# Four feed-forward chunks instead of two projected up by seven products, and one low part of each second pair formed by VectorE

## The chip, the cores and the metric

The kernel runs on one core of a Trainium2 chip. The core has TensorE (PE in the rows of the profile) for matrix products into PSUM, VectorE (DVE), ScalarE (ACT) and GpSimd (POOL) for element-wise work, and DMA queues that SyncE (SP), ScalarE and GpSimd start. Each engine works through its own instructions in program order and waits for the others on semaphores. The metric is the device time of one execution in microseconds (us), the median over several runs; lower is better.

## The reference

The program is a trunk of two layers over a sequence of 512 tokens with 1024 channels, all in float32. Each layer is wrapped by two feed-forward networks (FFNs), so the program has four of them:

```python
def swiglu_ffn(x, w_gu, w_d):
    g, u = jnp.split(x @ w_gu, 2, axis=-1)
    return (jax.nn.silu(g) * u) @ w_d
...
for i in range(DEPTH):                       # DEPTH = 2
    x = layer_norm(DN_ALPHA * x + 0.5 * swiglu_ffn(x, ffn1_wgu[i], ffn1_wd[i]), ...)
    mix = mlstm_mixer(...) if i % 2 == 0 else gmlp_mixer(...)
    x = layer_norm(DN_ALPHA * x + mix, ...)
    x = layer_norm(DN_ALPHA * x + 0.5 * swiglu_ffn(x, ffn2_wgu[i], ffn2_wd[i]), ...)
    ...                                      # gated per-layer embedding, one more layer_norm
```

The hidden width is 2816, that is 22 blocks of 128. The up projection `x @ w_gu` makes a gate block and an up block of columns for each hidden block; the down projection takes the product back to 1024 channels. Only the FFNs are touched here.

## The kernel before

**Products.** Each float32 operand is split into a high part (rounded to the matmul format, `whi`, by ScalarE, L274) and a low part (`wlo`, the rest). A product is three matmuls: high by high, high by low, low by high (`mm3`, L387 to L389; L389 takes the low part of the weights in the up projection and the low part of `h` in the down projection).

**Chunks.** `ffn` walks over the hidden blocks in six chunks of 2, 4, 4, 4, 4 and 4 blocks (`FFN_CHUNKS`); they are called chunk 0 to chunk 5 below. While a chunk is projected up, the chunk before it is projected down; the down projection always goes by seven products of half-size pieces (`Group`, tile `gps`), whose results are added to the residual `xt` by VectorE (L760, L762) at each step.

**Two ways up.** Chunks 0 to 3 are projected up plainly (tile `sup` in the staged beginning, `fps` after it): for each of the 8 column blocks of a four-block chunk 8 x 3 matmuls of 512 columns. ScalarE's and VectorE's work for one column block is a split of its weights (high on ACT, low on DVE at L283), and after it the SiLU or the product with the gate. Chunks from `UP_FROM` = 4 on go by seven products (`UpForms`, `UpPair`, tile `ups`): two hidden blocks make a pair, a pair is a 2 by 2 arrangement (gate and up columns by two halves of the channels), and seven products of 24 matmuls with 256 columns take the place of eight, after Strassen and Winograd. A chunk has a first and a second pair, so products 0 to 13; after each odd one comes a `gps` product of the down projection.

**What the seven products need.** On the side of the activations seven combinations of quarters of x are formed once for an FFN (tiles `x_a`, `x_f`, `x_d`, `t`, `t_f`, all on VectorE with splits by ScalarE). This is done in the chunk before the first chunk that uses them, two steps after each column block from the third on (`FORM_AT` = 2). On the side of the weights each pair needs four VectorE sums or differences in place (L139, L140 for the third product, L147, L148 for the fifth), on quarters of 512 KB that SyncE loads into `wbox`.

**Low parts.** Of a pair's seven low parts five are made by a DMA (`UP_BY_DMA` = 1, 3, 4, 5, 6): ScalarE writes minus the rounded weights into `wlo` (L280) and a DMA that GpSimd issues (L281) adds the weights to it. The third of them, number 4, is that of the fifth product, whose form is made at L147 and L148. The other two low parts are VectorE subtractions (L289 in these chunks). They are put off: `fill` makes the high part and leaves the low part in `pending`, and `lows` issues it one product later.

**Order.** The order is written out by hand: `W.order` lists the weights in the order of use, `fill` splits the next one when one of four `main` buffers is released after a product, and each engine's program is what these calls emit. A load into a freed quarter waits for the low part that was the quarter's last reader.

**Affine in chunk 1.** Where the norm ahead of an FFN left its gain and shift for later (FFN 2, 3 and 4, not FFN 1), VectorE applies them to `xt` at L754 and L755, once at the end of chunk 0 and three times in the first steps of chunk 1.

Of the kernel before, what the change touches and what calls it, by code (L numbers as in the profile page):

```python
# [17 lines left out]
P = 128  # L18
# [5 lines left out]
HID = 2816  # L24
# [19 lines left out]
EXTRA = 2  # L44
PLE_EXTRA = 3
UP_BY_DMA = (1, 3, 4, 5, 6)


class Weights:
# [75 lines left out]
        self.after.update({t2: (made[0][1],), t1: (made[1][1], t2)})  # L125
        return [(kind, js, make) for js, make in made]

    def up_forms(self, j11, j12, j21, j22):

        vec, raws = self.nc.vector, self.raws  # L130

        def a11():
            return raws[j11], ()

        def a12():
            return raws[j12], ()

        def s2():
            vec.tensor_add(raws[j21], raws[j21], raws[j22])  # L139
            vec.tensor_sub(raws[j11], raws[j21], raws[j11])  # L140
            return raws[j11], ()

        def s1():
            return raws[j21], (j21,)

        def s3():
            vec.tensor_sub(raws[j12], raws[j12], raws[j11])  # L147
            vec.tensor_sub(raws[j11], raws[j22], raws[j11])  # L148
            return raws[j11], (j11,)

        def s4():
            return raws[j12], (j12,)

        def a22():
            return raws[j22], (j22,)

        made = [((j11,), a11), ((j12,), a12), ((j21, j22), s2), ((), s1), ((), s3), ((), s4), ((), a22)]
        for _, make in made:
            self.in_place.add(make)
        self.after.update({s2: (a11,), s3: (a12, s2)})  # L160
        self.by_dma.update(made[r][1] for r in UP_BY_DMA)
        return [("main", js, make) for js, make in made]

    def spare(self, kind):
# [192 lines left out]
def hybrid_trunk(ctx: ExitStack, tc, x, p, ln_g, ln_b, ffn1_wgu, ffn1_wd, ffn2_wgu, ffn2_wd,  # L357
# [87 lines left out]
    def kp(w):  # L445
        return w.rearrange("(kb p) c -> p kb c", p=P)
# [4 lines left out]
    def add_pairs(w, a0, b0):  # L451

        W.add((w_cols(w, a0), cols2), (w_cols(w, b0), cols2))
# [4 lines left out]
    def add_rows(w, kb, n, kind="main"):  # L458
        for k in range(0, n, 2):
            W.add((kp(w)[:, kb + k:kb + k + 2, :], rows2), kind=kinds_of(kind, k))  # L460
# [7 lines left out]

    FFN_CHUNKS = [2, 4, 4, 4, 4, 4]
    LAST = len(FFN_CHUNKS) - 1  # L470
    UP_FROM = 4
    FORM_AT = 2
    turn_p = []

    def ffn_weights(wgu, wd, name, ple=False):
        starts = [sum(FFN_CHUNKS[:c]) for c in range(LAST + 1)]

        def forms(c):
            m = FFN_CHUNKS[c] // 2

            def quarter(i, j):
                k = starts[c] + m * i
                return kp(wd)[:, k:k + m, j * 512:(j + 1) * 512]
            loads = [W.add_load(quarter(i, j), n, name) for i, j, n in ((0, 0, 2), (0, 1, 1), (1, 1, 1), (1, 0, 2))]
            return W.forms("rows", *((j, slice(None)) for j in loads))

        first = len(W.order)
        for at in range(starts[UP_FROM]):
            if at == 0 or at == starts[UP_FROM] - 1:
                W.add(*((kp(wgu)[:, :, c0:c0 + P], [slice(None)]) for c0 in (at * P, HID + at * P)))  # L490
            elif at % 2:
                add_pairs(wgu, at * P, HID + at * P)
        tiles = W.order[first:]
        del W.order[first:]
        for c, n in enumerate(FFN_CHUNKS):
            down_w = deque(forms(c - 1) if c else ())
            if c >= UP_FROM:
                products = []
                for b in range(starts[c], starts[c] + n, 2):
                    products += W.up_forms(*(W.add_load(kp(wgu)[:, k:k + 4, c0:c0 + 2 * P], 1, "box")  # L500
                                             for c0 in (b * P, HID + b * P) for k in (0, 4)))
                for s, product in enumerate(products):
                    W.order.append(product)
                    if s % 2:
                        W.order.append(down_w.popleft())
                continue
            for i in range(2 * n):
                W.order.append(tiles[2 * starts[c] + i])
                if down_w:
                    W.order.append(down_w.popleft())  # L510
        if ple:
            W.add_hook("rows", lambda hi, lo: turn_p.pop()(hi, lo))
        add_rows(wd, starts[LAST], 4, ["rowsx", "rows", "main", "main"] if ple else ["main", "rows", "rowsx", "rows"])
# [74 lines left out]
    def ple_weights(i):  # L588
        add_rows(ple_wp[i], 0, 2)
        add_wide(ple_wg[i], 0, ["extra", "extra", "extra", "main"])  # L590
        add_wide(ple_wg[i], 512, ["rows", "rows", "rowsx", "rows2"])

    ffn_weights(ffn1_wgu[0], ffn1_wd[0], (0, 0))
    ml_weights()
    ffn_weights(ffn2_wgu[0], ffn2_wd[0], (0, 2), True)
    ple_weights(0)
    ffn_weights(ffn1_wgu[1], ffn1_wd[1], (1, 0))
    gm_weights()
    ffn_weights(ffn2_wgu[1], ffn2_wd[1], (1, 2), True)
# [108 lines left out]
    class Norm:  # L708
# [18 lines left out]
        def prepare(self, t):  # L727
            mv = small.tile([P, 2], F32, name="mv", tag="mv")
            vec.bn_aggr(mv, self.st[t])
            rs = small.tile([P, 2], F32, name="rs", tag="rs")  # L730
            vec.tensor_scalar(rs[:, 0:1], mv[:, 1:2], EPS, None, op0=OP.add)
            pool.tensor_tensor(rs[:, 1:2], rs[:, 0:1], eps_pow, op=OP.pow)
            self.rs[t] = mv[:, 0:1], rs[:, 1:2]
# [374 lines left out]
    def ffn(layer, k, rows, late, prepare=None):  # L1108
        with stage_pool("forms", 2) as fpool, stage_pool("quarters", Q_BUFS) as qpool, \
# [17 lines left out]
            def up_products(c, n, h):  # L1127
                nonlocal norm
                for s in range(7 * n // 2):
# [13 lines left out]
                    W.lows()  # L1143
                    if c == UP_FROM and s in formed.last:
                        formed.last[s]()
# [19 lines left out]
            for c, n in enumerate(FFN_CHUNKS):  # L1165
                if c < LAST:
                    h = hpool.tile([P, 4, SEQ], F32, name="h", tag="h")[:, :n]
                elif prepare is not None:
                    prepare()
                if c == UP_FROM - 1:  # L1170
                    formed = UpForms(tpool, late)
                W.apart = c >= UP_FROM
                if c >= UP_FROM:
# [776 lines left out]
```

## Time and profile before

| | |
|---|---|
| median of 3 runs | 2241.99 us (2235.75 to 2245.25) |
| the profiled execution | 2245.95 us, its span 2244.2 us |
| PE busy | 2205.9 us of the span, 98% |
| DVE busy | 1675.5 us, 75% |
| ACT busy | 1076.6 us, 48% |
| granted TensorE clock, mean | 0.992 |
| adding DMAs `wlo<-wbox` | 80, 512 KB each, median 5.9 us from issue to landing |

The page's row of an engine gives busy time, share of the span and number of instructions. A row of the view by windows gives the window from the span's start and its length, then for each engine the busy time and, in brackets, the instructions in it, then the granted TensorE clock (1.00 is full), the mean busy share of the DMA engines, and GB/s. A row of the timeline gives start, duration, engine, line, operation, `output<-inputs`, shapes, and in square brackets the idle time before it and what ended it. Consecutive matmuls overlap, so their cost is the distance of their starts, and a busy PE is not a PE at its peak. In the text "FFN 1" to "FFN 4" are the four FFNs in the order of time; FFN 2's chunk 1 begins at 799.63 us, its chunk 4 at 977.82.

### The profile page before, as it was taken

The page shows a single profiled execution, that of the slowest core. Times are in us where ns is not written, and L with a number is a line of the kernel's source. Part 1 is how long each engine was busy: PE and PEld are TensorE (multiplying, and loading weights), DVE is VectorE, ACT ScalarE, POOL GpSimd, SP SyncE. Part 2 cuts the span into 40 slices and gives each one's busy share as a digit, 9 for nine tenths or more (in the row PEclk, how much of TensorE's full clock was granted, in tenths as well). Part 3 has the DMA queues.
Part 4 walks back from the last instruction along what each step waited for, and adds up shares of the span by engine and source line. Part 5 has one row for each costly group of instructions (what it writes and reads, how often), then busy time and mean ns, then how long its engine had stood idle before and what let it go on. Part 6 is the DMA issues. An engine that isn't in the chain of part 4 may idle for free.

```text
span 2244.2 us, 29572 instructions
## 1 busy us (share of the span) xinstructions
PE 2205.9 (98%) x11669; PEld 1900.9 (85%) x11669; DVE 1675.5 (75%) x2436; ACT 1076.6 (48%) x1508; POOL 172.5 (8%) x215
## 2 busy tenths in 40 slices
PE   9999999999999999999999999999999999999998
PEld 8888988888888888888888888898888888888987
DVE  5668877786767776697786768886788767678887
ACT  3334655464646433356444334665345553336642
POOL 1000110111101100001000000110001100001100
PEclk9999999999999999999999999999999999999999
DMA  6334864456847432267632334764437743336651
GB/s 194 105 99 132 185 147 138 104 137 136 155 127 150 132 127 91 89 153 171 173 127 67 113 103 121 189 137 137 141 93 140 162 140 113 103 113 139 156 176 57
DMA packets 218355, 295.71 MB, mean 132 GB/s; under 512 B 7604, under 2 KB 162356, under 8 KB 218216
## 3 DMA queue, kind: packets, MB, share of 16 engines
q1 hardware_dynamic: 168592, 211.83, 29.3%
q0 software_dynamic: 43008, 67.30, 18.5%
q10 hardware_dynamic: 6616, 14.69, 1.9%
q8 instruction: 92, 1.51, 0.3%
q14 instruction: 47, 0.39, 0.0%
HBM read 224.58 MB, written 2.11 MB: 101 GB/s over the span
## 4 chain that ended last, share of the span: by engine, by line
PE 76%; DVE 11%; ACT 5%; DMA 4%; issue 3%; POOL 0%; SPq 0%; DVEq 0%; POOLq 0%; ACTq 0%
PE fps L387 7%; PE fps L388 7%; PE fps L389 7%; PE gps L387 5%; PE gps L388 5%; PE gps L389 5%; DMA wlo<-wbox 3%; PE dps L388 2%; PE dps L389 2%; PE dps L387 2%; DVE wlo L289 2%; PE ups L389 2%; PE ups L387 2%; PE ups L388 2%; ACT whi L274 1%
## 5 line engine op out<-in xcount | busy, mean ns | idle before, releaser
L274 ACT ACTIVATE whi<-wraw 128x1024 fp32r<-128x1024 f32 (+1 forms) x276 | 283.2, 1045 | 95.5 <-DVE wraw L118 22.5
L387 PE MATMUL fps<-xh,whi 128*128 128x512 f32 x800 | 311.4, 389 | 0.0
L388 PE MATMUL fps<-xl,whi 128*128 128x512 f32 x800 | 311.2, 389 | 0.0
L389 PE MATMUL fps<-xh,wlo 128*128 128x512 f32 x800 | 311.2, 389 | 0.0
L283 DVE TENSOR_TENSOR wlo<-wraw,whi 128x1024 fp32r<-128x1024 f32 (+1 forms) x204 | 245.0, 1215 | 48.8 <-ACT whi L274 48.0
L387 PE MATMUL gps<-whi,fhi 128*128 128x512 f32 x644 | 252.8, 393 | 0.0
L388 PE MATMUL gps<-wlo,fhi 128*128 128x512 f32 x644 | 252.3, 392 | 0.0
L389 PE MATMUL gps<-whi,flo 128*128 128x512 f32 x644 | 251.8, 391 | 0.0
L274 ACT ACTIVATE whi<-wquarter 128x1024 fp32r<-128x1024 f32 (+1 forms) x140 | 135.7, 969 | 213.1 <-PE gps L389 136.4
L283 DVE TENSOR_TENSOR wlo<-wquarter,whi 128x1024 fp32r<-128x1024 f32 (+1 forms) x92 | 97.6, 1061 | 151.9 <-ACT whi L274 151.9
L762 DVE TENSOR_TENSOR xt<-xt,gps 128x512 f32<-128x512 f32 x302 | 193.5, 679 | 5.5 <-PE gps L389 5.5
L274 ACT ACTIVATE whi<-wbox 128x1024 fp32r<-128x1024 f32 x112 | 117.9, 1052 | 131.5 <-DVE wbox L140 63.6
L389 PEld LDWEIGHTS fps<-xh,wlo 128*128 128x128 f32 x800 | 150.2, 188 | 31.5
L387 PEld LDWEIGHTS fps<-xh,whi 128*128 128x128 f32 x800 | 150.2, 188 | 31.0
L388 PEld LDWEIGHTS fps<-xl,whi 128*128 128x128 f32 x800 | 150.2, 188 | 30.9
L389 PE MATMUL ups<-xh,wlo 128*128 128x256 f32 x512 | 150.5, 294 | 22.1 <-DMA wlo<-wbox 22.1
L281 POOL DMA_DIRECT2D wlo<-wbox x80 | 68.0, 850 | 1170.6 <-ACT wlo L280 968.9
L387 PE MATMUL ups<-xh,whi 128*128 128x256 f32 x512 | 149.5, 292 | 0.4
L388 PE MATMUL ups<-xl,whi 128*128 128x256 f32 x512 | 149.0, 291 | 0.0
L389 PEld LDWEIGHTS gps<-whi,flo 128*128 128x128 f32 x644 | 121.3, 188 | 26.5
L387 PEld LDWEIGHTS gps<-whi,fhi 128*128 128x128 f32 x644 | 122.0, 189 | 24.0
L388 PEld LDWEIGHTS gps<-wlo,fhi 128*128 128x128 f32 x644 | 121.7, 189 | 23.7
(365 smaller groups left out, 5203.3 us busy)
## 6 DMA issues: line engine op xcount, KB each, us to landing
wraw<-in_ffn_wgu_dram SPq DMA_DIRECT2D x47, 1024.0 KB, 6.7
wlo<-wbox POOLq DMA_DIRECT2D x80, 512.0 KB, 5.9
wquarter<-in_ffn_wd_dram SPq DMA_DIRECT2D x64, 512.0 KB, 3.8
wbox<-in_ffn_wgu_dram SPq DMA_DIRECT2D x64, 512.0 KB, 5.5
wraw<-in_ml_w_in_dram SPq DMA_DIRECT2D x24, 1024.0 KB, 5.6
wlo<-wraw POOLq DMA_DIRECT2D x48, 512.0 KB, 6.4
wraw<-in_gm_w_in_dram SPq DMA_DIRECT2D x15, 1024.0 KB, 5.7
wraw<-in_ffn_wgu_dram SPq DMA_DIRECT2D x17, 512.0 KB, 4.9
```

Source lines behind the costliest of these rows:

```text
L274: self.nc.scalar.activation(hi[:, s], src[:, s], AF.Copy)
L281: self.nc.gpsimd.dma_start(lo[:, s], src[:, s], accum_op=OP.add)
L283: self.nc.vector.tensor_sub(lo[:, s], src[:, s], hi[:, s].bitcast(F32))
L289: self.nc.vector.tensor_sub(lo, src, hi.bitcast(F32))
L387: mm(ps, st[0], mv[0], start=start, stop=False, skip_group_check=more)
L388: mm(ps, st[0], mv[1], start=False, stop=False, skip_group_check=more)
L389: mm(ps, st[1], mv[0], start=False, stop=stop, skip_group_check=more)
L762: vec.tensor_add(dst, dst, ps)
```

## The change

Chunks 2 and 3 of each FFN are now projected up by seven products too (`UP_FROM` = 2), so chunks 2 to 5. The combinations of x are therefore formed in chunk 1 instead of chunk 3. In the second pair of every such chunk the low part of the fifth product is no longer made by the DMA but by a subtraction on VectorE (`UP_BY_DMA_2`); the first pair keeps its five DMAs.

```diff
 UP_BY_DMA = (1, 3, 4, 5, 6)
+UP_BY_DMA_2 = (1, 3, 5, 6)
...
-    def up_forms(self, j11, j12, j21, j22):
+    def up_forms(self, j11, j12, j21, j22, by_dma=UP_BY_DMA):
...
-        self.by_dma.update(made[r][1] for r in UP_BY_DMA)
+        self.by_dma.update(made[r][1] for r in by_dma)
...
     FFN_CHUNKS = [2, 4, 4, 4, 4, 4]
     LAST = len(FFN_CHUNKS) - 1
-    UP_FROM = 4
+    UP_FROM = 2
     FORM_AT = 2
...
                 for b in range(starts[c], starts[c] + n, 2):
                     products += W.up_forms(*(W.add_load(kp(wgu)[:, k:k + 4, c0:c0 + 2 * P], 1, "box")
-                                             for c0 in (b * P, HID + b * P) for k in (0, 4)))
+                                             for c0 in (b * P, HID + b * P) for k in (0, 4)),
+                                            by_dma=UP_BY_DMA if b == starts[c] else UP_BY_DMA_2)
```

The two added lines move the line numbers of what follows by one or two. The first place is ScalarE in the second pair of FFN 2's first seven-product chunk, from the fourth product's weights to the sixth's. Before (`wlo<-wbox` is the negated copy that the DMA adds to):

```order
L274 ACTIVATE whi<-wbox 128x1024
L280 ACTIVATE wlo<-wbox 128x1024
L1084 ACTIVATE us<-ups 128x512
L274 ACTIVATE whi<-wbox 128x1024
L280 ACTIVATE wlo<-wbox 128x1024
L274 ACTIVATE whi<-wquarter 128x1024
L940 ACTIVATE fhi<-h 128x512
L274 ACTIVATE whi<-wbox 128x1024
L280 ACTIVATE wlo<-wbox 128x1024
```

and now:

```order
L275 ACTIVATE whi<-wbox 128x1024
L281 ACTIVATE wlo<-wbox 128x1024
L1086 ACTIVATE us<-ups 128x512
L275 ACTIVATE whi<-wbox 128x1024
L275 ACTIVATE whi<-wquarter 128x1024
L942 ACTIVATE fhi<-h 128x512
L275 ACTIVATE whi<-wbox 128x1024
L281 ACTIVATE wlo<-wbox 128x1024
```

The copy between the fifth product's high part and the next weights is gone, and with it one DMA of GpSimd.

The second place is VectorE at the same point, from the two operations that form the fifth product's weights. Before:

```order
L147 TENSOR_TENSOR wbox<-wbox 128x1024
L148 TENSOR_TENSOR wbox<-wbox 128x1024
L762 TENSOR_TENSOR xt<-xt,gps 128x512 x2
L1087 TENSOR_TENSOR us<-us,ups 128x512
L943 TENSOR_TENSOR flo<-h,fhi 128x512
L289 TENSOR_TENSOR wlo<-wquarter,whi 128x1024
```

and now:

```order
L148 TENSOR_TENSOR wbox<-wbox 128x1024
L149 TENSOR_TENSOR wbox<-wbox 128x1024
L764 TENSOR_TENSOR xt<-xt,gps 128x512 x2
L1089 TENSOR_TENSOR us<-us,ups 128x512
L945 TENSOR_TENSOR flo<-h,fhi 128x512
L290 TENSOR_TENSOR wlo<-wbox,whi 128x1024
L290 TENSOR_TENSOR wlo<-wquarter,whi 128x1024
```

The subtraction `wlo<-wbox,whi` stands behind the low part of `h` and ahead of the low part of a down weight.

The third place is VectorE in chunk 1 of FFN 2, from the last of the affine operations on. Before:

```order
L755 TENSOR_TENSOR xt<-xt,gb 128x1024
L760 SCALAR_TENSOR_TENSOR xt<-xt,gps 128x512 x2
L1191 SCALAR_TENSOR_TENSOR h<-sg,fps 128x512
L283 TENSOR_TENSOR wlo<-wquarter,whi 128x512
L283 TENSOR_TENSOR wlo<-wraw,whi 128x1024
L943 TENSOR_TENSOR flo<-h,fhi 128x256
L760 SCALAR_TENSOR_TENSOR xt<-xt,gps 128x512 x2
```

and now:

```order
L757 TENSOR_TENSOR xt<-xt,gb 128x1024
L1001 TENSOR_TENSOR x_a<-xh,xl 128x512 x2
L1001 TENSOR_TENSOR x_f_7631<-xh,xl 128x1024
L762 SCALAR_TENSOR_TENSOR xt<-xt,gps 128x512 x2
L1193 SCALAR_TENSOR_TENSOR h<-sg,fps 128x512
L284 TENSOR_TENSOR wlo<-wquarter,whi 128x512
L284 TENSOR_TENSOR wlo<-wraw,whi 128x1024
L945 TENSOR_TENSOR flo<-h,fhi 128x256
L1013 TENSOR_TENSOR x_f_7631<-x_a,x_f_7631 128x512 x2
L1001 TENSOR_TENSOR x_f_7632<-xh,xl 128x1024
L762 SCALAR_TENSOR_TENSOR xt<-xt,gps 128x512 x2
```

The combinations of x now stand between the steps of chunk 1, right behind the affine operations; the remaining ones follow in the same way up to the end of chunk 1 and into chunk 2. In the whole program PE has 12405 rows instead of 11253, and GpSimd's adding DMAs from `wbox` go from 80 to 144.

## The prediction

> **What bounds the kernel now.** I read the page's engine shares first, then the chain that ended last, then windows around single chunks, then the waits of TensorE.
>
> ```profile
> PE 2205.9 (98%) x11669; PEld 1900.9 (85%) x11669; DVE 1675.5 (75%) x2436; ACT 1076.6 (48%) x1508; POOL 172.5 (8%) x215
> PE 76%; DVE 11%; ACT 5%; DMA 4%; issue 3%; POOL 0%; SPq 0%; DVEq 0%; POOLq 0%; ACTq 0%
> ```
>
> PE sets the end; a matmul less is time less, and everything else matters only where PE waits for it. The windows show what a chunk costs PE. First a plain four-block chunk (FFN 2, chunk 3) and its parts, one column block and one down product; then the same two parts in a seven-product chunk, two products (x48 matmuls) and one down product:
>
> ```profile
> core 0: us, PE busy (x) PEld busy (x) DVE busy (x) ACT busy (x) POOL busy (x), PEclk, DMA share, GB/s
> 915.26:977.82 62.56, 62.56 (x278) 51.80 (x277) 49.25 (x61) 23.58 (x29) 0.88 (x1) 1.00 0.34 101
> 972.38:977.82 5.44, 5.44 (x26) 4.50 (x25) 4.22 (x6) 1.58 (x2) 0.00 (x0) 1.00 0.00 0
> 1035.07:1040.82 5.75, 5.75 (x49) 5.75 (x48) 4.86 (x7) 3.16 (x4) 0.00 (x0) 1.00 0.65 155
> 1040.82:1043.57 2.75, 2.75 (x15) 2.26 (x13) 2.75 (x5) 2.01 (x2) 0.30 (x1) 1.00 0.00 0
> 1020.28:1031.76 11.48, 8.11 (x49) 7.91 (x48) 4.68 (x6) 7.48 (x10) 1.70 (x2) 0.75 1.02 230
> ```
>
> A plain chunk takes 62.56 us. A seven-product chunk has seven rounds of two products and one down product, so undisturbed 7 x (5.75 + 2.75) = 59.50 us. The last row is the round with products 10 and 11: the same 48 matmuls need 11.48 instead of 5.75 us, at a granted clock of 0.75 and with the DMA engines full (1.02). What the eight such chunks of the program really take (each FFN's chunks 4 and 5; the first, the fourth, the last, and the sum of all eight):
>
> ```profile
> 213.92:277.08 63.16, 61.14 (x421) 57.42 (x420) 52.10 (x65) 42.99 (x53) 8.41 (x10) 0.97 0.75 176
> 1043.57:1110.20 66.63, 62.31 (x429) 58.40 (x428) 46.56 (x59) 36.64 (x47) 7.34 (x9) 0.97 0.65 159
> 2088.72:2153.75 65.03, 62.37 (x430) 58.25 (x428) 47.80 (x60) 36.53 (x47) 7.64 (x9) 0.97 0.65 163
> sum 515.74, PE 491.84 PEld 460.69 DVE 402.24 ACT 319.60 POOL 64.43; mean PE 61.48 PEld 57.59 DVE 50.28 ACT 39.95 POOL 8.05
> 1100.99 0.87 PE ptp L1817 x8
> ```
>
> 515.74 - 8 x 59.50 = 39.7 us are lost. The last row, a piece of the chain, is other work in FFN 2's chunk 5, eight transposes with 0.87 us, and I count the same for FFN 4: about 38 us are stalls, 4.8 a chunk. So today a seven-product chunk is on average slower than a plain one (64.3 against 62.6). Where they stall:
>
> ```profile
> PE ups L389 <- DMA wlo<-wbox: 23.5, 9, 4.3
> 1018.91 7.95 DMA wlo<-wbox
> 1026.90 0.58 PE L389 MATMUL ups<-xh,wlo 128*128 128x256 f32 x1 [3.37 <-DMA wlo<-wbox]
> 1027.28 0.42 PE L387 MATMUL ups<-xh,whi 128*128 128x256 f32 x1
> 1027.49 0.41 PE L388 MATMUL ups<-xl,whi 128*128 128x256 f32 x1
> 2074.74 0.39 PE L389 MATMUL ups<-xh,wlo 128*128 128x256 f32 x1 [1.84 <-DMA wlo<-wbox]
> 2074.96 0.28 PE L387 MATMUL ups<-xh,whi 128*128 128x256 f32 x1
> 2075.08 0.28 PE L388 MATMUL ups<-xl,whi 128*128 128x256 f32 x1
> ```
>
> PE waits nine times, 23.5 us, for an adding DMA, and the one here is that of product 11, the second pair's fifth: issued at 1018.91, landed 7.95 us later, 3.4 us too late. What the wait row doesn't hold of the 38 us is what follows: after an idle time of 3.37 us the starts lie 0.21 us apart instead of 0.12, after 1.84 us they lie 0.12 apart.
>
> **Part 1, chunks 2 and 3 by seven products.** Eight more chunks (two in each of four FFNs) go from 62.56 to 59.50 us of PE work: 8 x 3.06 = **-24.5 us**, if they don't wait. Their VectorE work rises from the 40.3 us of a plain chunk to at most the 46.6 to 47.8 us of chunk 5 above (chunk 4's 52.1 holds the end of the x combinations) and one subtraction; against 59.5 us that is covered. ScalarE (43.0) is covered too. GpSimd gets 64 more DMAs of 0.85 us, and the DMA engines go from a share of 0.34 to about 0.75 there.
>
> **Part 2, the low part by VectorE.** It removes in each second pair ScalarE's copy, GpSimd's issue and a 512 KB DMA, and adds one subtraction:
>
> ```profile
> L289 DVE TENSOR_TENSOR wlo<-wbox,whi 128x1024 fp32r<-128x1024 f32 x24 | 29.2, 1218 | 0.0
> L280 ACT ACTIVATE wlo<-wbox 128x1024 fp32r<-128x1024 f32 x80 | 83.5, 1044 | 0.0
> ```
>
> Is it in time? In FFN 2's chunk 4 the next-standing low part, that of the down weight, ran behind `flo`. The new one takes its place:
>
> ```profile
> 1020.72 1.22 DVE L289 TENSOR_TENSOR wlo<-wquarter,whi 128x1024 fp32r<-128x1024 f32 x1
> ```
>
> It would end at 1021.94, or a microsecond sooner as ScalarE is freed of its copy ahead of `fhi`; product 11 wants it at 1026.90 - 3.37 = 1023.53. What stands behind it on VectorE, a low part of a down weight and two residual adds, moves by 1.2 us and is wanted a round later. So the stall of product 11 goes in all eight chunks: **-38 us**.
>
> What is late next are products 12 and 13, whose low parts still come by DMA. GpSimd issued them at:
>
> ```profile
> 1022.27 0.85 POOL L281 DMA_DIRECT2D wlo<-wbox  x1 [2.52 <-ACT wlo L280]
> 1025.17 0.84 POOL L281 DMA_DIRECT2D wlo<-wbox  x1 [2.04 <-DMA wlo<-wbox]
> wlo<-wbox POOLq DMA_DIRECT2D x80, 512.0 KB, 5.9
> 1085.02 8.81 DMA wlo<-wbox
> ```
>
> Without the stall PE wants them at 1020.28 + 5.75 + 2.75 + 0.24 = 1029.0 and, one product of 2.87 us on, 1031.9. That leaves 6.75 us from issue to landing, and up to 7.7 with ScalarE a copy ahead. The median is 5.9, the longest shown 8.8, both with the DMA that now goes still in flight beside them. Bounds per chunk: no wait, or 2 us; over sixteen chunks 0 to 32 us. The median is nearer, so I take **+5 us**.
>
> **Part 3, the x combinations in chunk 1.** They must be done in a chunk of 53 us instead of 62.6, and in FFN 2 to 4 behind the affine operations. The VectorE column of FFN 1's chunk 1 (no affine), FFN 2's chunk 1, the last part of it, and FFN 2's plain chunk 2:
>
> ```profile
> 46.64:99.68 53.04, 53.04 (x235) 43.92 (x234) 33.31 (x46) 18.51 (x26) 0.00 (x0) 1.00 0.38 120
> 799.63:852.69 53.06, 53.06 (x235) 43.92 (x234) 42.63 (x57) 17.97 (x26) 0.00 (x0) 1.00 0.37 119
> 829.50:852.69 23.19, 23.19 (x104) 19.18 (x103) 17.96 (x25) 8.57 (x11) 0.00 (x0) 1.00 0.46 150
> 852.69:915.26 62.57, 62.57 (x278) 51.80 (x277) 40.31 (x49) 21.39 (x26) 0.00 (x0) 1.00 0.29 93
> ```
>
> Forming them raised chunk 3 from 40.3 to 49.25, by 9 us. In FFN 2's chunk 1 that makes 42.6 + 9 = 51.6 of 53.1 us: no room for the waits in between. I followed VectorE in its new order from 829.50, where the first combination now stands, to the end of L149, the form of the first pair's fifth product. Rows that give the distance of starts, and the places to compare with:
>
> ```profile
> 829.50 1.28 DVE L760 SCALAR_TENSOR_TENSOR xt<-xt,gps 128x512 f32<-128x512 f32 x2
> 936.41 1.22 DVE L283 TENSOR_TENSOR wlo<-wraw,whi 128x1024 fp32r<-128x1024 f32 x1
> 937.55 0.68 DVE L943 TENSOR_TENSOR flo<-h,fhi 128x512 fp32r<-128x512 f32 x1
> 938.15 1.27 DVE L762 TENSOR_TENSOR xt<-xt,gps 128x512 f32<-128x512 f32 x2
> 985.91 1.23 DVE L148 TENSOR_TENSOR wbox<-wbox 128x1024 f32<-128x1024 f32 x1
> 989.48 0.86 POOL L281 DMA_DIRECT2D wlo<-wbox  x1 [8.34 <-PE ups L389]
> 995.01 0.28 PE L389 MATMUL ups<-xh,wlo 128*128 128x256 f32 x1
> 845.89 0.39 PE L387 MATMUL gps<-whi,fhi 128*128 128x512 f32 x1
> ```
>
> A 1024-wide operation takes 1.14 us to the next start (1.22 where that one needs its result; 1.17 on average), a 512-wide one 0.60, a 256-wide one half of that. The order has 15, 29 and 2 of them in this stretch: 17.6 + 17.4 + 0.6 = 35.6 us, and three waits for high parts of ScalarE, some 2.7 us by the 1.04 us that such a copy takes. It ends at 829.5 + 38.3 = 867.8, which is 15.1 us into chunk 2 if PE kept its pace. In FFN 2's chunk 4 it ended at 987.14, 9.3 us into it, and the low part that hangs on it, issued at 989.48, was just in time at 995.01: at most 5.5 us for a DMA with a median of 5.9. So VectorE is 5.8 us later, and of that a slack of at most about 1 us covers something. PE loses the other 5 us: 1.4 where the seventh down product (845.89) waits for the residual add two steps earlier, which by the same count ends at 847.3, and some 3.5 where product 4 waits for its DMA. The latter is long enough to halve the clock for a while, which costs about 1.5 us (16 products' starts at 0.21 instead of 0.12). Together 6.5 us in FFN 2, 3 and 4: **+19.5 us**. Bounds: nothing, if the waits shrink and slack covers it; 12 us each, if products 5 and 6 wait in turn, 36 in all. FFN 1 has 9.3 us less to do in chunk 1 and pays nothing.
>
> On the half clock the Trainium skill (TensorE: Matmul & The Clock Gate, on the clock gate) says that the clock falls after an idle window of about 3.4 us that runs free of the program. By that, a wait of 3.5 us may or may not halve the clock, and the sum would be up to 4.5 us lower. The trace has it after 3.37 us of waiting and not after 1.84.
>
> **Sum.** -24.5 - 38 + 5 + 19.5 = -38 us on 2245.95 us, the profiled execution's own time: 2208. That execution was 4 us above the median of the runs, and its stalls, which vary with the DMAs, are part of it; I take 2 us off: **2206 us**, 1.6% less than 2242.
>
> **The rivals.**
> - *VectorE in chunk 1 is no problem.* For it: VectorE had 5.2 us (23.19 - 17.96) of idle time between 829.5 and 852.69. Against it: 9 us of work have to go into it. Time: 2206 - 19.5 = 2187.
> - *Products 12 and 13 inherit the stall.* The margin is 0.9 to 1.8 us at the median and negative at the longest landing. 1.2 us in each of 16 chunks instead of 5 in all: 2206 + 14 = 2220.
> - *VectorE stays behind through chunk 2.* Products 4, 5 and 6 all wait for DMAs that queue behind each other; 12 us an FFN instead of 6.5: 2206 + 17 = 2223.
> - *Slower: the stall belongs to the second half of the chunk, not to that one DMA.* The DMA engines are at 1.02 there; if the remaining DMAs simply land late, sixteen chunks lose what eight lose today, 4.8 us each, with chunk 1's loss on top: 2246 - 24.5 - 38 + 16 x 4.8 + 19.5 = 2280. It turns slower than before at 16 x = 24.5 + 38 - 19.5, that is from 2.7 us a chunk. Against it: one of three overlapping DMAs is taken away.
> - *The change doesn't do what it says:* the subtraction stands behind `flo` and is itself late by some 2 us; sixteen chunks lose 2.5 us: 2246 - 24.5 - 38 + 40 + 19.5 = 2243, no change.
>
> **How the numbers follow.** Forecast 0.45, no trouble in chunk 1 0.15, products 12 and 13 0.14, VectorE behind 0.13, slower 0.08, no change 0.05. The forecast's own range is 2196 to 2216. The first four are faster by more than 0.5% (about what a measurement here tells from no change): 0.87; same 0.05, slower 0.08. The range goes from 2181, a little under the second case, to 2236.
>
> **What would show it.** In the changed profile: seven-product chunks near 59.5 us, the round of products 10 and 11 at 5.75 us with no wait for the DMA; a first wait in FFN 2 to 4 around the end of chunk 1 and at product 4 of chunk 2, with half clock behind it, and none in FFN 1. The prediction is wrong if chunks 3 to 5 lose over 2 us each to products 12 and 13, if chunk 1 and 2 lose nothing or over 10 us, or if a middle chunk turns out bound by VectorE.

## The result, and the profile after

The median of four runs is 2214.16 us (2213.62 to 2217.81), against 2242.47 us for the kernel before: a ratio of 0.988, 95% interval 0.986 to 0.991. That is 28 us less where 36 were forecast. The profiled execution took 2217.81 us, its span 2216.1, so 28.1 us less than the span before. The page's rows of engines (PE has 1152 instructions more than before) and of the chain that ended last:

```profile
PE 2179.8 (98%) x12821; PEld 1928.9 (87%) x12821; DVE 1762.2 (80%) x2532; ACT 1209.0 (55%) x1668; POOL 227.2 (10%) x279
PE 80%; DVE 10%; ACT 4%; issue 3%; DMA 2%; SPq 0%; POOL 0%; DVEq 0%; ACTq 0%; POOLq 0%
```

TensorE still sets the end, and DMAs have half their earlier share of the chain. The windows show FFN 2's chunks 2, 4 and 5 in this order, the rounds of products 10 and 11 in chunks 2, 4 and 5, FFN 1's chunk 5 and the rest of its down projection behind it, and FFN 2's chunk 1 together with the last column block of chunk 0 (from the first `fps` product on):

```profile
842.29:908.35 66.06, 61.75 (x422) 57.22 (x421) 58.65 (x72) 43.52 (x54) 7.95 (x10) 0.97 0.69 167
967.78:1027.21 59.43, 59.43 (x421) 55.97 (x420) 49.94 (x60) 38.85 (x47) 7.63 (x10) 1.00 0.74 177
1027.21:1088.91 61.70, 60.56 (x429) 56.85 (x428) 47.62 (x60) 35.70 (x46) 6.50 (x8) 1.00 0.64 158
891.37:897.12 5.75, 5.75 (x50) 5.74 (x49) 3.43 (x5) 5.10 (x7) 1.31 (x2) 1.00 0.91 225
1010.24:1015.99 5.75, 5.75 (x50) 5.75 (x49) 2.52 (x3) 3.91 (x5) 0.86 (x1) 1.00 1.07 271
1069.67:1075.42 5.75, 5.75 (x50) 5.75 (x49) 3.65 (x5) 5.75 (x9) 1.70 (x2) 1.00 0.62 152
267.94:328.67 60.73, 59.69 (x421) 56.03 (x420) 46.48 (x56) 35.47 (x44) 6.45 (x8) 1.00 0.60 145
328.67:356.62 27.95, 26.22 (x117) 20.93 (x116) 21.01 (x35) 12.45 (x25) 1.67 (x3) 0.94 0.39 139
782.80:842.29 59.49, 59.05 (x260) 48.27 (x259) 49.03 (x66) 20.30 (x30) 0.88 (x1) 1.00 0.41 126
```

The middle chunk takes 59.43 us, all of it busy, and chunk 3 and those of the other FFNs take the same. The round that took 11.48 us in the first seven-product chunk takes 5.75 in all sixteen, with the DMA engines nearly as full in the first (0.91) and full in a middle one (1.07). Chunk 2 takes 66.06 us: longer than the plain chunk it replaces. The same two stretches of the kernel before that answer to the last two rows:

```profile
343.99:368.01 24.02, 24.02 (x117) 19.89 (x116) 19.06 (x32) 11.80 (x24) 1.67 (x3) 1.00 0.31 105
794.18:852.69 58.51, 58.51 (x260) 48.44 (x259) 44.04 (x59) 19.82 (x29) 0.00 (x0) 1.00 0.42 136
```

Cutting the whole span at the starts of the chunks in the same way gives this ledger, in us:

| stretch | before, FFN 1 to 4 | after, FFN 1 to 4 | difference |
|---|---|---|---|
| chunk 1, with chunk 0's last column block | 58.6, 58.5, 58.5, 58.5 | 58.6, 59.5, 59.5, 59.5 | +2.9 |
| chunk 2 | 62.57 each | 61.2, 66.1, 67.0, 67.0 | +11.0 |
| chunk 3 | 62.57 each | 59.43 each | -12.5 |
| chunk 4 | 63.2, 65.8, 63.8, 61.5 | 59.43 each | -16.5 |
| chunk 5 | 66.9, 66.6, 63.0, 65.0 | 60.7, 61.7, 60.7, 60.8 | -17.7 |
| down projection after it | 24.0, 24.9, 23.7, 24.9 | 28.0, 24.9, 25.6, 25.0 | +5.9 |

These are -26.9 of the -28.1 us; most of the rest lies ahead of FFN 1's first `fps` product, which starts at 29.2 us instead of 30.2. TensorE's waits after (instruction waiting, what it waited for, total us, times, longest):

```profile
PE ups L388 <- ACT us L1086: 12.8, 7, 3.3
PE dps L389 <- DVE wlo L290: 5.0, 4, 1.6
PE ups L390 <- DMA wlo<-wbox: 3.3, 4, 1.1
```

The 23.5 us of waits for an adding DMA have become 3.3, and a wait that did not exist before leads the list: a product of the up projection (`ups`) waits for ScalarE's copy `us`, which takes an earlier product's result out of PSUM. The timeline of TensorE shows it at product 4 of chunk 2, in FFN 2 (where the first row is the last matmul of product 2) and in FFN 3:

```profile
855.10 0.28 PE L390 MATMUL ups<-t_whi,wlo 128*128 128x256 f32 x1
...
860.58 0.39 PE L390 MATMUL gps<-whi,flo 128*128 128x512 f32 x1
864.28 0.39 PE L388 MATMUL ups<-xh,whi 128*128 128x256 f32 x1 [3.31 <-ACT us L1086]
865.48 0.42 PE L388 MATMUL ups<-xh,whi 128*128 128x256 f32 x1
865.70 0.42 PE L389 MATMUL ups<-xl,whi 128*128 128x256 f32 x1
...
1272.83 0.58 PE L388 MATMUL ups<-xh,whi 128*128 128x256 f32 x1 [3.33 <-ACT us L1086]
```

After the wait the starts lie 0.21 us apart instead of 0.12: in FFN 3 up to 1278.4, in FFN 4 likewise. That is half clock (the granted clock is 0.50 from 1271.58 to 1278.41, so it began within the wait), and it costs some 2.5 us on top of the wait; in FFN 2 it begins later, at 865.4, and costs some 1.5. Now the same moment on VectorE (the first row: the end of the form of the fifth product's weights), on ScalarE, and on GpSimd's queue with the landing time of its DMA:

```profile
855.56 1.23 DVE L149 TENSOR_TENSOR wbox<-wbox 128x1024 f32<-128x1024 f32 x1
```

```profile
856.82 1.06 ACT L275 ACTIVATE whi<-wbox 128x1024 fp32r<-128x1024 f32 x1 [3.69 <-DVE wbox L149]
857.78 1.05 ACT L281 ACTIVATE wlo<-wbox 128x1024 fp32r<-128x1024 f32 x1
...
862.19 1.04 ACT L275 ACTIVATE whi<-wquarter 128x1024 fp32r<-128x1024 f32 x1
863.13 0.61 ACT L942 ACTIVATE fhi<-h 128x512 fp32r<-128x512 f32 x1
863.65 0.58 ACT L1086 ACTIVATE us<-ups 128x512 f32<-128x512 f32 x1
```

```profile
859.13 0.86 POOL L282 DMA_DIRECT2D wlo<-wbox  x1 [10.65 <-ACT wlo L281]
wlo<-wbox POOLq DMA_DIRECT2D x1, 512.0 KB, 4.5
```

ScalarE stood idle for 3.69 us, because the next instruction in its queue was the high part of weights that VectorE had not formed yet. Then it worked without a gap through what was queued behind (four rows are left out), and last came the copy out of PSUM. It takes the result of product 2, done at 855.4, from the bank to which product 4 adds next, so it was ready for 8 us before it began at 863.65. The DMA of product 4 landed at 863.7, itself 2.7 us after TensorE was free (861.0); the copy ended at 864.2.

### The profile page after: what moved, and what is told of

It reads as the page before. It is cut to its first block, busy times and chain, and to the rows that moved or that the text cites. A ratio compares the mean times of both kernels' runs of the same rounds, so it can differ in the third digit from the quotient of the medians.

```text
span 2216.1 us, 32537 instructions
## 1 busy us (share of the span) xinstructions
PE 2179.8 (98%) x12821; PEld 1928.9 (87%) x12821; DVE 1762.2 (80%) x2532; ACT 1209.0 (55%) x1668; POOL 227.2 (10%) x279
## 4 chain that ended last, share of the span: by engine, by line
PE 80%; DVE 10%; ACT 4%; issue 3%; DMA 2%; SPq 0%; POOL 0%; DVEq 0%; ACTq 0%; POOLq 0%
PE ups L388 8%; PE ups L390 8%; PE ups L389 8%; PE gps L388 7%; PE gps L389 7%; PE gps L390 7%; PE dps L389 2%; PE dps L390 2%; PE dps L388 2%; DVE wlo L284 2%; ACT whi L275 1%; PE gups L388 1%; PE vps L388 1%; PE zps L388 1%; PE zps L390 1%
## 5 line engine op out<-in xcount | busy, mean ns | idle before, releaser
L275 ACT ACTIVATE whi<-wbox 128x1024 fp32r<-128x1024 f32 x224 | 235.9, 1054 | 229.6 <-DVE wbox L141 101.6
L388 PE MATMUL ups<-xh,whi 128*128 128x256 f32 x1024 | 293.1, 286 | 11.5 <-ACT us L1086 11.5
L390 PE MATMUL ups<-xh,wlo 128*128 128x256 f32 x1024 | 293.0, 286 | 3.3 <-DMA wlo<-wbox 3.3
L389 PE MATMUL ups<-xl,whi 128*128 128x256 f32 x1024 | 292.6, 286 | 0.0
L388 PEld LDWEIGHTS ups<-xh,whi 128*128 128x128 f32 x1024 | 199.3, 195 | 15.4 <-ACT us L1086 13.2
L390 PEld LDWEIGHTS ups<-xh,wlo 128*128 128x128 f32 x1024 | 199.2, 195 | 4.1 <-DMA wlo<-wbox 4.1
L389 PEld LDWEIGHTS ups<-xl,whi 128*128 128x128 f32 x1024 | 199.4, 195 | 2.3
L281 ACT ACTIVATE wlo<-wbox 128x1024 fp32r<-128x1024 f32 x144 | 150.3, 1044 | 0.0
L290 DVE TENSOR_TENSOR wlo<-wquarter,whi 128x1024 fp32r<-128x1024 f32 x104 | 126.7, 1218 | 0.0
L388 PE MATMUL fps<-xh,whi 128*128 128x512 f32 x288 | 112.2, 390 | 0.0
```

Source lines behind the costliest of these rows:

```text
L275: self.nc.scalar.activation(hi[:, s], src[:, s], AF.Copy)
L281: self.nc.scalar.activation(lo[:, s], src[:, s], AF.Copy, scale=-1.0)
L290: self.nc.vector.tensor_sub(lo, src, hi.bitcast(F32))
L388: mm(ps, st[0], mv[0], start=start, stop=False, skip_group_check=more)
L389: mm(ps, st[0], mv[1], start=False, stop=False, skip_group_check=more)
L390: mm(ps, st[1], mv[0], start=False, stop=stop, skip_group_check=more)
```

## The experiments

Each edit below is made to the changed kernel, and each ratio is to the kernel before.

**Where does the old stall live?** My theory: with the adding DMA, product 11 is late in every seven-product chunk. The rival: the subtraction matters little, and the stall went because the chunks follow each other differently. First part 1 alone: four chunks, all second pairs with the DMA.

```diff
-                                            by_dma=UP_BY_DMA if b == starts[c] else UP_BY_DMA_2)
+                                            by_dma=UP_BY_DMA)
```

> Chunks 2 to 5 by seven products, but all second pairs keep the DMA for the fifth product's low part. Theory (the stall of product 11 belongs to that DMA and comes back in every seven-product chunk that has it): sixteen stalls instead of the eight of before, some 3 to 5 us each, on top of the changed kernel's 2214 us: 2214 + 16 x 4 = 2278 us, at least 2250, so slower than before; the round of products 10 and 11 is 8 to 12 us long in all of chunks 2 to 5. Rival (the stall went because the chunks follow each other differently, the subtraction matters little): about 2214 to 2225 us.

Measured: 2229.8 us against 2241.6, ratio 0.995 (0.993 to 0.997). Windows of FFN 4's chunks 2, 3 and 5, and TensorE's largest wait:

```profile
1886.55:1956.77 70.22, 63.48 (x422) 58.61 (x421) 57.28 (x71) 44.46 (x55) 8.81 (x11) 0.95 0.71 165
1956.77:2016.34 59.57, 59.57 (x422) 56.01 (x420) 46.45 (x56) 38.40 (x47) 8.19 (x10) 1.00 0.81 193
2075.77:2138.07 62.30, 61.09 (x429) 56.96 (x428) 47.29 (x60) 36.76 (x47) 7.35 (x9) 1.00 0.66 165
...
PE ups L390 <- DMA wlo<-wbox: 13.9, 9, 2.4
```

A middle chunk keeps all its DMAs and stalls nowhere; the old stall is found in the first seven-product chunk (a wait of up to 2.4 us at product 11) and, at product 13, in the last. My theory fell, and the time lies above the rival's range too. What the trace suggests is a third reading: the stall comes only where the form of the weights is late. Why the middle chunk escapes is a matter of when the DMA is issued, here GpSimd's row in the middle chunk, with its time to the landing:

```profile
1995.10 0.86 POOL L282 DMA_DIRECT2D wlo<-wbox  x1 [4.75 <-ACT wlo L281]
wlo<-wbox POOLq DMA_DIRECT2D x1, 512.0 KB, 7.2
```

In the middle chunk it landed at 2002.3, 45.5 us into the chunk; product 11 wants it about 45.6 us in. Before, in the first seven-product chunk, it was issued 41.1 us into the chunk, 2.8 us later than here (38.3), with a landing time of 7.95 us. VectorE's form, on which the issue hangs, ends 38.7 us into the first such chunk before, 39.0 into the last, and 35.9 into a middle one here. So the stall is there when the forms run late, and just not there when they don't; how long the DMA takes decides with it, for in the last chunk of this run the form is as late (39.0 to 39.1), but the DMA landed after 4.5 to 5.0 us, and product 11 waits at most 0.43 us.

Then part 2 alone (`UP_FROM` back at 4):

```diff
-    UP_FROM = 2
+    UP_FROM = 4
```

> Only chunks 4 and 5 by seven products, as before, with the subtraction on VectorE in the second pairs. Theory (the gain of the change is the removed stall; what the eight further chunks save, 8 x 3.1 = 25 us, is paid back by VectorE being late at the end of chunk 1 and in chunk 2, 24.7 us in FFN 2 to 4 and 1.8 us in FFN 1): the same time as the changed kernel, 2210 to 2220 us, and no wait in chunk 4. Rival (the two parts need each other, or the further chunks carry the gain): 2225 to 2242 us.

Measured: 2215.3 us (2214.4 to 2217.8), ratio 0.989 (0.987 to 0.990), the whole gain of the full change. Part 1 adds nothing to it: what chunk 3 and chunk 2's shorter work bring (-25) is paid back at chunks 1 and 2. And the two parts alone (-11.8, -26.3) give more together than the change does, since each shortens chunks 4 and 5; part 1 does so above all because chunk 4 is then no longer the first of its kind.

Last, the subtraction only where the stall was seen, in the first and the last seven-product chunk:

```diff
+                                            by_dma=UP_BY_DMA if b == starts[c] or UP_FROM < c < LAST else UP_BY_DMA_2)
```

> The changed kernel with the subtraction on VectorE only in the first and the last seven-product chunk (2 and 5); in chunks 3 and 4 the second pair's fifth low part goes back to the DMA. Theory, as the run with all of them by DMA left chunks 3 and 4 at 59.4 to 59.6 us: the same time as the changed kernel, 2211 to 2218 us; the stall needs a late form of the fifth product's weights, which only the first and the last chunk have. Rival (chunks 3 and 4 were spared there because the stalls ahead of them gave them time): a wait of 1 to 4 us at product 11 in chunks 3 and 4, 2222 us or more.

Measured: 2214.62 us, ratio 0.989 (0.987 to 0.990): the same as the change. The middle chunks took 59.43 to 59.56 us. So in the two middle chunks the subtraction wins nothing, and the stalls ahead of them were not what spared them: the reading by late forms fits every chunk, though no run makes the form of a middle chunk late to test it.

**Where did part 1's gain go?** Theory: VectorE's added work in chunk 1 makes chunk 2 late. The rival: any first seven-product chunk loses this much. One chunk less:

```diff
-    UP_FROM = 2
+    UP_FROM = 3
```

> Chunks 3 to 5 by seven products, the combinations of x formed in chunk 2, which is 62.6 us long and has no affine operations. Theory (the loss in chunks 1 and 2 is VectorE having both in a short chunk): four chunks give up 3.1 us each, 12.5 us, and FFN 2 to 4 lose nothing at the first seven-product chunk, 24.7 us back: 2214 - 24.7 - 1.8 + 12.5 = 2200 us. Rival (the loss belongs to the first seven-product chunk wherever it stands, as it starts up the DMAs): 2214 + 12.5 = 2226 us.

Measured: 2196.95 us (2195.3 to 2198.4), ratio 0.980 (0.979 to 0.982): 17 us faster than the change with four product chunks fewer. FFN 1's chunks 3 and 5 and the down projection:

```profile
150.31:211.02 60.71, 60.01 (x422) 56.08 (x420) 54.98 (x67) 41.96 (x52) 7.88 (x10) 1.00 0.76 182
270.45:329.88 59.43, 59.43 (x421) 55.98 (x420) 48.15 (x59) 36.01 (x45) 6.45 (x8) 1.00 0.64 159
329.88:353.90 24.02, 24.02 (x117) 19.89 (x116) 19.13 (x32) 11.82 (x24) 1.67 (x3) 1.00 0.40 135
```

The first chunk loses 1.1 to 1.3 us (60.55 to 60.71 us in the four FFNs), not 7: where the combinations of x have a longer chunk without affine operations, the loss is nearly gone. The rival fell.

Is it the affine operations? The next kernel leaves the gain and shift ahead of FFN 2 to 4 out of the computation, four steps on VectorE in each:

```diff
-        if norm.deferred:
+        if norm.deferred and norm.at // KB % 4 == 0:
```

> The changed kernel without the gain and shift that VectorE applies to the residual at the beginning of FFN 2, 3 and 4 (left out of the computation there). Theory (VectorE is late because these 9 us stand in chunk 1 together with the combinations): chunk 2 of FFN 2 to 4 becomes like that of FFN 1, 61.2 us instead of 66 to 67, and the time falls by 3 x 7 = 20 us to 2194. Rival (the wait for ScalarE's copy at product 4 comes from ScalarE's own order, not from VectorE): chunk 2 stays at 65 us or more and the time falls by less than 6 us.

Measured: 2198.13 us, one run. And one that leaves nothing out, but moves two of the three affine steps of chunk 1 into chunk 0, so that chunk 1 has one:

```diff
-                    if c == 1 and i < 3:
+                    if c == 0 and i % 2 or c == 1 and i < 1:
```

> The changed kernel with two of the four affine operations of FFN 2 to 4 moved from chunk 1 into chunk 0, so that only one of them (2.4 us of VectorE) stands in chunk 1; the computation is whole. Theory (chunk 2's loss is VectorE's backlog at the end of chunk 1, us for us, until a floor as in FFN 1): 4.8 us less backlog in each of three FFNs, chunk 2 from 66 to 67 down to 61.2 to 62, in all 2214 - 3 x 5 = 2199 us. Rival (VectorE is full in chunk 0 too and carries the backlog on): no more than 4 us gained, 2210 us or above.

Measured: 2200.17 us (2200.1 to 2200.4), ratio 0.982 (0.981 to 0.983). A third begins the combinations one column block earlier as well (`FORM_AT` = 1):

> As the run before it, and the combinations of x begin one column block earlier in chunk 1. Theory: they need 15 us of VectorE and end 6 to 7 us earlier, so product 4 of chunk 2 no longer waits in FFN 1 (1.5 us) nor in the others: chunk 2 near 59.5 us, 2190 to 2195 us in all. Rival (what holds product 4 is VectorE's total work in chunk 1, not the order in it): within 3 us of the run before it.

Measured: 2201.04 us, ratio 0.983 (0.981 to 0.984). FFN 3's chunk 2 in these three, in this order, one fence for each kernel:

```profile
1243.26:1304.50 61.24, 59.70 (x422) 55.90 (x421) 55.80 (x69) 42.07 (x52) 7.93 (x10) 1.00 0.74 179
```

```profile
1243.44:1305.44 62.00, 59.95 (x422) 55.94 (x420) 56.56 (x70) 42.10 (x53) 7.93 (x10) 1.00 0.73 178
```

```profile
1241.29:1304.72 63.43, 61.18 (x421) 57.37 (x420) 56.03 (x67) 43.52 (x54) 7.93 (x10) 0.97 0.72 174
```

Against 66.97 us in the change, 5.7, 5.0 and 3.5 us are won by taking three affine steps or two out of chunk 1. So the loss comes from VectorE's work in chunk 1, and the affine steps are what overfills it. Beginning the combinations earlier doesn't help FFN 2 to 4: their wait at product 4 is 2.25 us there and at most 1.8 without it. It does help FFN 1, whose chunk 2 fell from 61.2 to 59.43 us. There the place of the work was at fault; where VectorE's chunk is full, less work helped and an earlier start did not.

**What exactly does product 4 wait for?** My forecast said the adding DMA; the trace says ScalarE's copy. If the DMA sets the wait, forming that low part of chunk 2 by VectorE removes it; if it is ScalarE's queue, the wait for the copy stays.

```diff
-                                            by_dma=UP_BY_DMA if b == starts[c] else UP_BY_DMA_2)
+                                            by_dma=UP_BY_DMA if b == starts[c] and c > UP_FROM else UP_BY_DMA_2)
```

> The changed kernel, with the low part of product 4 in chunk 2 (the first pair's fifth product) made by VectorE too, so that no DMA stands between its form and product 4. The prediction's step (PE waits for that DMA): chunk 2 of FFN 2 to 4 falls from 66 to 67 us by about the DMA's 4.5 us plus the clock's 1.5, to 61 us. Theory from the trace (PE waits for ScalarE's copy out of the PSUM bank, which stands in ScalarE's order behind the high part of product 4 and so behind VectorE's late form): chunk 2 stays at 65 to 68 us and product 4 still ends a wait of 3.3 us for that copy; 2211 to 2218 us in all.

Measured: 2211.46 us, one run. TensorE's row at product 4, and ScalarE's at the same point:

```profile
861.35 0.39 PE L388 MATMUL ups<-xh,whi 128*128 128x256 f32 x1 [2.49 <-ACT us L1086]
...
854.72 1.06 ACT L275 ACTIVATE whi<-wbox 128x1024 fp32r<-128x1024 f32 x1 [3.69 <-DVE wbox L149]
860.72 0.58 ACT L1086 ACTIVATE us<-ups 128x512 f32<-128x512 f32 x1
```

The wait is 2.49 us instead of 3.31, for the same copy, and ScalarE has the same 3.69 us gap behind the same form. The wait is 0.82 us shorter, which my expectation did not have; the negated copy that falls out of the queue (1.05 us long in the change) would account for it. It is ScalarE's queue.

**The last chunk.** In FFN 1 product 12 and the down projection lost 5.2 us together. The DMA pieces of the chain there, after (the third is the like product in FFN 2), with SyncE's row for the last two loads of down weights:

```profile
311.81 8.45 DMA wlo<-wbox
320.39 6.04 DMA wraw<-in_ffn_wd_dram
1071.08 9.44 DMA wlo<-wbox
311.56 9.21 SPq L239 DMA_DIRECT2D wraw<-in_ffn_wd_dram  x2
```

A 1 MB load starts at 311.56, beside product 12's adding DMA, which then takes 8.45 us; the second load starts only at 320.39, and the down projection waits for it. That DMA is also issued later here than in a middle chunk, 43.9 us into the chunk instead of 40.8: in FFN 3's chunk 4 the same DMA took 9.4 us, and nothing waited. With three seven-product chunks (the kernel with `UP_FROM` = 3) the same two loads, and product 12's DMA with its landing time, read:

```profile
289.43 30.15 SPq L239 DMA_DIRECT2D wraw<-in_ffn_wd_dram  x2
314.32 0.85 POOL L282 DMA_DIRECT2D wlo<-wbox  x1 [7.78 <-ACT wlo L281]
wlo<-wbox POOLq DMA_DIRECT2D x1, 512.0 KB, 4.8
```

There the first load is 25 us earlier, the DMA without a load beside it takes 4.8 us, and neither product 12 nor the down projection waits. Such a load needs a whole free 1 MB buffer. So I loaded the last four blocks of down weights as quarters of 512 KB:

```diff
-        add_rows(wd, starts[LAST], 4, ["rowsx", "rows", "main", "main"] if ple else ["main", "rows", "rowsx", "rows"])
+        for k, to in enumerate(["rowsx", "rows", "main", "main"] if ple else ["main", "rows", "rowsx", "rows"]):
+            j = W.add_load(kp(wd)[:, starts[LAST] + k:starts[LAST] + k + 1, :], 1, "box")
+            W.order.append((to, (j,), lambda j=j: (W.raws[j], (j,))))
```

> The changed kernel, with the last four blocks of the down weights loaded as four quarters of 512 KB into the quarter slots instead of two loads of 1 MB that need a whole free slot. Theory (in the last chunk the first of these loads starts only 43.6 us into the chunk, runs beside product 12's adding DMA, which then lands after 8.4 us, and the second comes too late for the down projection): the loads start earlier, the waits of product 12 in chunk 5 (1.0, 1.1, 1.0 and 0.2 us) go, and so does the longer wait at the beginning of the down projection in FFN 1 and 3 (3.9 and 2.0 us more than before): 2214 - 8 = 2206 us. Rival (those DMAs are slow because the adding DMAs fill the DMA engines by themselves): 2213 to 2216 us.

Measured: 2222.84 us, ratio 0.992 (0.990 to 0.994): 9 us slower than the change, and above both ranges. TensorE's two largest new waits:

```profile
PE sup L869 <- DVE wlo L284: 5.4, 2, 5.1
PE pwp L389 <- DVE wlo L284: 3.9, 4, 1.8
```

The mechanism was right: the last chunks fell by 4.4 us in all, the down projections of FFN 1 and 3 by 4.6, as expected. But the stages behind the FFNs, whose weights now come later, wait some 11 us and in part run at half clock afterwards, and that costs 13 us in the trace. In the trace that leaves a loss of some 4 us, near the 2.9 us between the spans (2219.0 against 2216.1); the medians of all executions are 9 us apart, which the two traces alone don't show.

**Versions.** The best of what was found, three seven-product chunks with the combinations one column block earlier (`UP_FROM` = 3, `FORM_AT` = 1):

> Chunks 3 to 5 by seven products (2197 us with the combinations from the third column block of chunk 2 on), the combinations one column block earlier. Theory (what the first seven-product chunk still loses, 1.1 to 1.3 us in each FFN, is VectorE and ScalarE coming late out of the chunk before): 2197 - 4 x 1.2 = 2192 us. Rival (it is DMAs landing late, whatever VectorE does): 2196 to 2198 us.

Measured: 2194.02 us (2194.0 to 2195.6), ratio 0.979 (0.978 to 0.981). It beats both kernels. FFN 3's first seven-product chunk, and TensorE's largest wait:

```profile
1303.08:1362.52 59.44, 59.44 (x422) 55.97 (x420) 52.65 (x64) 41.95 (x52) 7.94 (x10) 1.00 0.76 185
PE dps L389 <- DVE wlo L290: 1.8, 2, 0.9
```

This version with the quarter loads of above:

> Chunks 3 to 5 by seven products, the combinations one column block earlier (2194 us) and the quarter loads of the run before this one. Theory: there the first of the 1 MB loads started 19 us into the last chunk and neither product 12 nor the down projection of FFN 1 and 3 waits, so little is left: 2191 to 2195 us; at most the 0.9 us waits of the down projection in FFN 2 and 4 go. Rival (earlier loads displace others): 2197 us or more.

Measured: 2209.91 us, ratio 0.987 (0.984 to 0.990). There was nothing left for the quarters to win, and their price at the stages behind was the same 13 us in the trace: the rival, that earlier loads displace others, held.

## Why the prediction was right, and where not

The forecast, 2206 us, was 8 us too low; the direction and the main terms were right.

- **Part 1** (-24.5): 8 x (62.57 - 59.43) = -25.1 us. Right.
- **Part 2** (-38): chunks 4 and 5 took 515.7 us before. Eight times 59.43 and the two pieces of other work make 477.2, so 38.5 us of stall were there to be removed, and product 11 waits nowhere now. The size is right. The reason was too simple: I took the stall as a property of that DMA in every seven-product chunk, and it needs late forms, as in the first and the last chunk. The forecast didn't suffer, because the subtraction is made in every chunk; a forecast for part 1 alone did, by at least 20 us.
- **Products 12 and 13** (+5 over sixteen chunks): +4.4 us, but all of it at product 12 in the four last chunks and none in the twelve others. The sum fits by luck of the spread; what makes it is the later issue in the last chunk and the load that starts beside the DMA.
- **Part 3** (+19.5 in FFN 2 to 4, nothing in FFN 1): +24.7, and +1.8. This is the step that was mis-sized. VectorE's count in FFN 2 was good: L149 was to end 15.1 us into chunk 2 and ended 14.5 us into it (856.8). The wait at product 4 was forecast with 3.5 us and is 3.3. What failed is what I let follow. I asked only who needs the weights, and gave the wait to the adding DMA; behind the same late form stood ScalarE's queue, with the copy out of PSUM. It sets the wait at product 4 (the DMA, landing at 863.7 and wanted some 0.24 us into a product that could have begun at 861.0, would by estimate have left one of 2.4 us), and causes another one of 0.44 us earlier (chunk 1 and a late `flo` give 1.0 and 0.56 where 1.4 was forecast). Half clock cost 1.5 us in FFN 2, as forecast, but some 2.5 in FFN 3 and 4. In FFN 1, where I said that VectorE has the room, product 4 waits 1.54 us for the same copy, since the combinations begin too late there for ScalarE. The window that I took for FFN 1's chunk 1 was misplaced as well, by 11 us: the chunk runs from 35.76 to 88.80, with 33.85 us of VectorE instead of 33.31, so little hung on it.
- **Not foreseen**: the down projection after the last chunk, +5.9 us. I had asked of product 12's DMA only what other adding DMAs lie beside it, not when SyncE's 1 MB loads find a buffer.

Of the 10 us between the sum (-38) and the profiled difference (-28.1), 7 are Part 3 with FFN 1, and 6 the down projection; small gains of about 3 us go the other way. The rival by which the stall belongs to the second half of the chunk is refuted by the 5.75 us rounds of the first and the last seven-product chunk, those that stalled; that the subtraction itself is late, by the same rows. The round in a middle chunk, under full DMA engines, says nothing of it, since those chunks don't stall with the DMA either.

The Trainium skill (TensorE: Matmul & The Clock Gate, "Architectural detail", on the queues) calls ScalarE's queue strictly first in, first out. The trace agrees: while a copy was ready from 855.4 on, ScalarE stayed idle until 856.82 for an instruction ahead of it that was not.

## What to carry to other kernels

Where an instruction becomes late, follow the in-order queue of the engine that waits for it, and ask first what stands behind it that empties PSUM: here that stopped TensorE for longer (to 864.2) than the late operand would have (863.7). Cost the first and the last pass of a loop apart from the middle ones; here all that was lost lay in them, and the best version gave up one of the four passes. A transfer's time depends on what starts beside it, so ask when a large load will find its buffer, and what is loaded next when it finds it earlier.

## What the runs showed of the hardware

Half clock can follow waits well under 3.4 us, and need not follow a wait of 3.3. After 2.25 us at product 4 (the kernel with `FORM_AT` = 1 and early affine) FFN 3's chunk has a mean clock of 0.97, as after 2.50 us in the kernel without the adding DMA of that product. After 1.8 us in the sibling with `FORM_AT` = 2 the clock is 0.97 in FFN 2 and 1.00 in FFN 3 and 4. In the down projection of FFN 1 a wait of 1.60 us was enough (its window has 0.94), and one of 1.61 us in FFN 3 was not. In the kernel with the subtraction in the first and the last chunk alone, product 4 waits 3.3 us in FFN 2 and in FFN 3, and of these two only FFN 2 pays half clock behind it: its chunk 2 takes 66.07 us, FFN 3's 65.23.

What differs is where the wait lies in a fixed grid. Every slow stretch between the start and the end of the program is 3.41 or 6.83 us long in these traces, and within one trace they start whole multiples of 3.413 us apart, whatever the waits: in the change at 865.40, 1271.58 and 1899.64, that is 119 and 303 steps behind the first. Cut along this grid, the slice ahead of a slow stretch has TensorE busy for about half of it or less. First FFN 2's product 4 in the change, where the wait falls into one slice; then FFN 3's in the kernel just named, where it falls into two:

```profile
861.98:865.40 3.42, 1.12 (x9) 1.12 (x10) 1.94 (x3) 3.42 (x6) 0.84 (x1) 1.00 0.93 174
865.40:868.81 3.41, 3.41 (x18) 3.41 (x18) 3.38 (x5) 2.15 (x3) 0.86 (x1) 0.50 1.06 249
```

```profile
1265.56:1268.98 3.42, 1.55 (x7) 0.94 (x5) 2.87 (x5) 3.42 (x5) 1.34 (x2) 1.00 0.71 135
1268.98:1272.39 3.41, 1.95 (x16) 1.96 (x17) 2.45 (x4) 3.41 (x6) 0.08 (x1) 1.00 1.05 172
```

With 1.12 us busy of 3.42 the next slice runs at 0.50; with 1.55 and 1.95 it doesn't. There is no sharp limit in these figures: 1.69 us in the slice ahead of the slow one in FFN 1's down projection was too little. So a wait of 2 us should be priced with its chance of half clock behind it.

An adding DMA of 512 KB took 4.5 to 4.8 us from issue to landing with no load beside it, even where two of them overlapped (both 4.8 at 314.32 and 317.21 in the kernel with `UP_FROM` = 3). With a 512 KB load of weights starting beside it it took 7.2 us (at 1995.10 with part 1 alone) and 8.4 (at 1932.81), and beside a 1 MB load 8.45 and 9.44.

What stays open: why the last loads find their buffer 25 us earlier with three seven-product chunks than with four was read from the trace, not tried. No run puts ScalarE's copy out of PSUM ahead of the high part that is late, which would leave product 4 to the adding DMA. And the 1.0 us won ahead of FFN 1 has no cause that the traces show.
